# Seven block products in place of eight in the gate and up stages of a two-layer decoder trunk

## The chip, the cores and the metric

One core of one Trainium2 chip runs the whole program. The metric is device time in microseconds of one execution; three runs of the kernel before have a median of 978.27 us. All tensors are float32 in memory. The engines named below are TensorE (PE, matmuls, and PEld for its weight loads), VectorE (DVE), ScalarE (ACT), GpSimd (POOL) and SyncE (SP, which issues the weights' loads). Each engine works through its own instructions in the order in which the program emits them; semaphores hold an instruction until what it reads is there.

## What is computed

The reference is a trunk of two layers over 256 tokens of width 1024. Each layer is: half a gated feed-forward, a mixer (attention, short convolution and a recurrent branch), and half a second gated feed-forward, each behind an RMS norm. What matters here is the feed-forward:

```python
def swiglu(x, w_gate, w_up, w_down):        # w_gate, w_up: 1024 x 2816
    return (jax.nn.silu(x @ w_gate) * (x @ w_up)) @ w_down
...
h = x + 0.5 * swiglu(rms_norm(x, ffn1_norm[l]), ffn1_gate[l], ffn1_up[l], ffn1_down[l])
```

There are four of these (two in each layer), so four gate and up stages. The mixer's attention adds a relative bias whose table is spread over rows by a round trip through device memory.

## The kernel before

**Halves.** A float32 matmul is made of three fast ones: every operand is held as a high part, rounded to the matmul's format, and the remainder as a low part. `high` (L159) copies a weight piece to its high part on ACT, `low` (L164) subtracts on DVE. `mm3` (L203) issues the three matmuls. A piece is 512 KB, 128 x 1024 elements, loaded by SP into one of RAW = 6 buffers; PARTS = 7 pairs of high and low parts exist, so the splitting runs up to seven pieces ahead of TensorE.

**Order.** `pump` (L184) is called after each piece is used and calls `split` (L175): the high part of piece n, then the low part of piece n - 1. What is emitted for DVE after a `pump` thus stands behind the low parts of pieces that TensorE needs only six or seven pieces later.

**A gate and up stage** (`up_gate`, L300) has eleven units, each of 256 hidden columns: 256 gate columns and 256 up columns side by side, so 512 columns a matmul. A unit takes four pieces, each with 12 matmuls (two rows of 128 tokens, two blocks of 128 inputs, three products), 48 in all. After its last piece, `gate` (L313) forms silu(gate) on ACT and the product on DVE (L319), both scaled by the norm's factor of the token, since the matmuls take the input without that factor. `turn` (L324) transposes the result on TensorE (four transposes, L328) and splits it (ACT L330, DVE L331). It stands after the second piece of the next unit: TensorE comes to these transposes 24 matmuls after the unit's end.

**The norm's factor** is formed at the end of unit 0 (`ssq`, L243). In the first stage `ssq` stands in unit 2.

**Bias rows.** In the first stage `skew_out(i)` (L462, a copy of 384 KB from two partitions to device memory) and `skew_in(i)` (L470, back in another order) are issued on ACT's queue, after units 6 to 10: after unit 6 + i the copy out number i and the copy in number i - 1. A copy in waits for its copy out, and ACT's other work waits behind it.

Of the kernel before, what the change touches and what calls it, by code (L numbers as in the profile page):

```python
# [17 lines left out]
P = 128  # L18
DEPTH = 2
S = 256  # L20
# [10 lines left out]
RAW = 6  # L31
# [21 lines left out]
UNITS = KF // 2  # L53

# [16 lines left out]
def trunk(ctx: ExitStack, tc: tile.TileContext, t, out):  # L71
# [48 lines left out]
    pieces = []  # L120

    def four(w):

        pieces.extend((w[:, 0:4], w[:, 4:8]))

    for l in range(DEPTH):
        for f in ("ffn1", "ffn2"):
            pieces.extend(t[f"{f}_gu{l}"][i] for i in range(4 * UNITS))
            w = t[f"{f}_down{l}"]
            if l == DEPTH - 1 and f == "ffn2":  # L130
                pieces.extend(w[c, :, j:j + 1] for c in range(KF // 2) for j in range(2))
            else:
                pieces.extend(w[n, :, k0:k1] for n in range(4) for k0, k1 in DOWN_K)
# [6 lines left out]
    st = {"dma": 0, "split": 0, "low": 0, "use": 0, "done": 0}  # L140
    raws, parts = {}, {}

    def load(i, cut=1, before=None):
        src = pieces[i]
        r = raw_p.tile([P, src.shape[1], src.shape[2]], F32, tag="raw", name=f"raw{i}")
# [6 lines left out]
        raws[i] = r  # L152
        st["dma"] += 1

    def load_more():
        while st["dma"] < min(len(pieces), st["low"] + RAW):
            load(st["dma"])

    def high(i, s):  # L159
        if i not in parts:  # L160
            parts[i] = tuple(hl_p.tile(list(raws[i].shape), F32R, tag=g, name=f"{g}{i}") for g in ("wh", "wl"))
        nc.scalar.activation(out=parts[i][0][:, s], in_=raws[i][:, s], func=AF.Copy)  # L162

    def low(i, s):  # L164
        h, lo = parts[i]
        nc.vector.tensor_tensor(out=lo[:, s], in0=raws[i][:, s], in1=h[:, s].bitcast(F32), op=ALU.subtract)  # L166

    def low_to(n):
        while st["low"] < n:
            low(st["low"], slice(None))  # L170
            raws.pop(st["low"])
            st["low"] += 1
            load_more()

    def split():  # L175

        n = st["split"]
        if n >= len(pieces):
            return
        high(n, slice(None))  # L180
        st["split"] += 1
        low_to(n)

# [19 lines left out]
    def mm3(o, ah, al, bh, bl, first, last):  # L203
        nc.tensor.matmul(o, lhsT=ah, rhs=bh, start=first, stop=False)  # L204
        nc.tensor.matmul(o, lhsT=ah, rhs=bl, start=False, stop=False)  # L205
        nc.tensor.matmul(o, lhsT=al, rhs=bh, start=False, stop=last)  # L206
# [20 lines left out]
    def rows(o, w, k, ds):  # L227

        for d in ds:
            wh, wl = w[d // 2]  # L230
            mm3(o, xh[:, d, tok(k)], xl[:, d, tok(k)], wh[:, d % 2], wl[:, d % 2], d == 0, d == KD - 1)
# [68 lines left out]
    def up_gate(norm, first, hooks=()):  # L300

        hooks = dict(hooks)
        hid, tiles = [], []
        for j, n in enumerate((10, 8, 4)):
            tile_ = big.tile([P, n, 2, S], F32R, tag=f"A{j}", name=f"hid{j}")
            tiles.append((len(hid), tile_))
            hid += [tile_[:, k] for k in range(n)]

        def hidden(c):
            k0, tile_ = [x for x in tiles if x[0] <= 2 * c][-1]  # L310
            return tile_[:, 2 * c - k0:2 * c - k0 + 2]

        def gate(b):  # L313
            s = wk.tile([P, 2, 256], F32, tag="sg", name="sg")
            a = wk.tile([P, 2, 256], F32, tag="ga", name="ga")
            for k in range(2):
                nc.scalar.activation(out=s[:, k], in_=b[k][:, :256], func=AF.Silu, scale=norm.r[:, k:k + 1])  # L317
            for k in range(2):
                nc.vector.scalar_tensor_tensor(  # L319
                    out=a[:, k], in0=b[k][:, 256:], scalar=norm.r[:, k:k + 1], in1=s[:, k], op0=ALU.mult, op1=ALU.mult  # L320
                )
            return a

        def turn(c, a):  # L324
            b = bank("hT")
            for j in range(2):
                for k in range(2):
                    nc.tensor.transpose(b[:, (2 * j + k) * P:(2 * j + k + 1) * P], a[:, k, tok(j)], ident)  # L328
# [10 lines left out]
        for c in range(UNITS):  # L339
            b = pair("n")  # L340
            banks.append((c, b))
            if first and c == 0:
                start(b)
            else:
                for j in range(4):
                    w = [None] * j + take(1)
                    if j < 3 or c > 0:
                        for k in range(2):
                            rows(b[k], w, k, (2 * j, 2 * j + 1))
                    else:  # L350
                        for k in range(2):
                            rows(b[k], w, k, (KD - 2,))
                        rows(b[0], w, 0, (KD - 1,))
                        norm.ssq()
                        rows(b[1], w, 1, (KD - 1,))
# [5 lines left out]
                    if j > 0:  # L361
                        turn_next()
                    pump()
                    if first and c == 2 and j == 1:
                        gated += [(i, gate(o)) for i, o in banks[:2]]
                        banks = banks[2:]
            if not first or c > 1:
                gated += [(i, gate(o)) for i, o in banks]
                banks = []
            if c in hooks:  # L370
                hooks[c]()
        return hid, turn_next

    def ffn(norm, first, gain, hooks=()):
        hid, last = up_gate(norm, first, hooks)
        for n in range(4):
            acc = pair("d")
            for k0, k1 in DOWN_K:
                w = take(1)[0]
                for i in range(2):  # L380
                    c = slice(i * P, (i + 1) * P)
                    for k in range(k0, k1):
                        wide(acc[i], w[0][:, k - k0, c], w[1][:, k - k0, c], hid[k], k == 0, k == KF - 1)
# [3 lines left out]
                if n == 0 and k0 == 8:  # L387
                    last()
# [87 lines left out]

    def skew(i):
        def go():
            if i < 4:
                skew_out(i)  # L480
            if i > 0:
                skew_in(i - 1)
        return go
# [315 lines left out]
    for j in range(4):  # L799
        load(j, 2, lambda: load_x(j))  # L800
# [7 lines left out]
    def start(b):  # L808
# [3 lines left out]
        for j in range(4):  # L812
# [7 lines left out]
            raws.pop(j)  # L820
            parts.pop(j)
            st["use"] = st["split"] = st["low"] = st["done"] = j + 1
            load_more()
# [11 lines left out]
    ffn(norm, True, ("mix_norm", 0), once | {6 + i: skew(i) for i in range(5)})  # L835
    for l in range(DEPTH):
# [3 lines left out]
        if l < DEPTH - 1:  # L840
            ffn(norm, False, ("ffn1_norm", l + 1))
            norm = Norm()
            ffn(norm, False, ("mix_norm", l + 1))


    xn = big.tile([P, 2, D], F32, tag="A3", name="xn")

    def turn_back(k, n):
        def go():
            b = bank("xn")  # L850
            for i in range(4):
                nc.tensor.transpose(b[:, i * P:(i + 1) * P], xT[:, 4 * n + i, k * P:(k + 1) * P], ident)
            nc.scalar.activation(out=xn[:, k, n * 512:(n + 1) * 512], in_=b, func=AF.Copy)
        return go

    hid, turn_last = up_gate(norm, False, {2 + 2 * k + n: turn_back(k, n) for k in range(2) for n in range(2)})
# [7 lines left out]
    def row(k, n, w, d):  # L864
        c0, c1 = cuts[k][n]
        mm3(
            acc[k][n][:, :c1 - c0], hid[d][:, 0, tok(k)], hid[d][:, 1, tok(k)], w[0][:, 0, c0:c1], w[1][:, 0, c0:c1],
# [32 lines left out]
    for d in range(KF - 4):  # L900
# [5 lines left out]
        if d == 8:  # L906
            turn_last()
        pump()
# [17 lines left out]
def paired(g, u):  # L926

    both = np.concatenate([w.reshape(KD // 2, 2, P, UNITS, 256).transpose(3, 0, 2, 1, 4) for w in (g, u)], axis=-1)
    return np.ascontiguousarray(both.reshape(4 * UNITS, P, 2, 512))
# [34 lines left out]
```

## Time and profile before

| | |
|---|---|
| median of three runs | 978.27 us (977.99 to 981.36) |
| the profiled execution | 978.68 us, span 976.5 us |
| TensorE busy | 955.3 us, 98% of the span |
| VectorE busy | 581.4 us, 60% |
| ScalarE busy | 506.7 us, 52% |
| matmuls on TensorE | 5350 |

Busy shares are means over stages. Times below are microseconds from the start of the span; a matmul's shown duration is longer than the distance to the next one, because matmuls overlap.

### The profile page before, as it was taken

The page shows a single profiled execution, that of the slowest core. Times are in us where ns is not written, and L with a number is a line of the kernel's source. Part 1 is how long each engine was busy: PE and PEld are TensorE (multiplying, and loading weights), DVE is VectorE, ACT ScalarE, POOL GpSimd, SP SyncE. Part 2 cuts the span into 40 slices and gives each one's busy share as a digit, 9 for nine tenths or more (in the row PEclk, how much of TensorE's full clock was granted, in tenths as well). Part 3 has the DMA queues.
Part 4 walks back from the last instruction along what each step waited for, and adds up shares of the span by engine and source line. Part 5 has one row for each costly group of instructions (what it writes and reads, how often), then busy time and mean ns, then how long its engine had stood idle before and what let it go on. Part 6 is the DMA issues. An engine that isn't in the chain of part 4 may idle for free.

```text
span 976.5 us, 13921 instructions
## 1 busy us (share of the span) xinstructions
PE 955.3 (98%) x5350; PEld 830.9 (85%) x5350; DVE 581.4 (60%) x812; ACT 506.7 (52%) x775; POOL 24.1 (2%) x46
## 2 busy tenths in 40 slices
PE   8999969999999999999999999999999999999997
PEld 7788757899999888888888888888999988888886
DVE  6655425667788555555665555465778765555543
ACT  7555324556776544444544544444587655544441
POOL 0002000000000000000000000000001000000000
PEclk9999989999999999999999999999999999999999
DMA  8855447654445555646565555556444465555621
GB/s 308 271 179 197 145 146 215 222 170 171 138 143 200 198 188 187 205 152 195 169 220 181 185 173 183 162 187 221 159 143 157 160 210 192 183 182 182 221 93 44
DMA packets 53045, 176.64 MB, mean 181 GB/s; under 512 B 6867, under 2 KB 8948, under 8 KB 52980
## 3 DMA queue, kind: packets, MB, share of 16 engines
q1 hardware_dynamic: 48960, 171.46, 53.0%
q10 hardware_dynamic: 4020, 4.30, 1.5%
q8 instruction: 42, 0.69, 0.3%
q14 instruction: 23, 0.19, 0.1%
HBM read 173.11 MB, written 2.62 MB: 180 GB/s over the span
## 4 chain that ended last, share of the span: by engine, by line
PE 91%; DMA 6%; issue 1%; ACT 1%; ACTq 0%; DVE 0%; POOLq 0%; POOL 0%; SPq 0%
PE nb L204 8%; PE na L206 8%; PE na L204 8%; PE na L205 8%; PE nb L206 8%; PE nb L205 8%; PE da L221 6%; PE db L221 6%; DMA skew<-br 5%; PE da L222 3%; PE db L222 3%; PE hT L328 2%; PE v L204 1%; PE q L205 1%; PE wb L205 1%; PE wb L204 1%
## 5 line engine op out<-in xcount | busy, mean ns | idle before, releaser
L162 ACT ACTIVATE wh<-raw 128x1024 fp32r<-128x1024 f32 (+1 forms) x334 | 339.2, 1030 | 296.8 <-PE nb L206 106.9
L166 DVE TENSOR_TENSOR wl<-raw,wh 128x1024 fp32r<-128x1024 f32 (+1 forms) x334 | 387.9, 1187 | 66.7 <-ACT wh L162 66.7
L204 PE MATMUL na<-wh,xx 128*128 128x512 f32 x352 | 142.1, 404 | 1.4 <-ACT wh L162 1.4
L206 PE MATMUL na<-wh,xx 128*128 128x512 f32 x352 | 138.2, 393 | 0.0
L205 PE MATMUL na<-wl,xx 128*128 128x512 f32 x352 | 137.9, 392 | 0.2 <-DVE wl L166 0.2
L204 PE MATMUL nb<-wh,xx 128*128 128x512 f32 x352 | 137.9, 392 | 0.0
L206 PE MATMUL nb<-wh,xx 128*128 128x512 f32 x352 | 137.4, 390 | 0.0
L205 PE MATMUL nb<-wl,xx 128*128 128x512 f32 x352 | 137.4, 390 | 0.0
L331 DVE TENSOR_TENSOR hid<-hT,hid 128x512 fp32r<-128x512 f32 x44 | 30.4, 692 | 150.2 <-ACT hid L330 150.2
L221 PE MATMUL da<-hid,wh 128*128 128x512 f32 x252 | 92.4, 399 | 1.5 <-DVE hid L331 1.5
L221 PE MATMUL db<-hid,wh 128*128 128x512 f32 x252 | 92.1, 398 | 0.0
L204 PEld LDWEIGHTS na<-wh,xx 128*128 128x128 f32 x352 | 66.6, 189 | 14.3 <-ACT wh L162 1.6
L206 PEld LDWEIGHTS na<-wh,xx 128*128 128x128 f32 x352 | 66.5, 189 | 14.3
L205 PEld LDWEIGHTS nb<-wl,xx 128*128 128x128 f32 x352 | 66.4, 189 | 14.0
L206 PEld LDWEIGHTS nb<-wh,xx 128*128 128x128 f32 x352 | 66.4, 189 | 14.1
L204 PEld LDWEIGHTS nb<-wh,xx 128*128 128x128 f32 x352 | 66.4, 189 | 13.9
L205 PEld LDWEIGHTS na<-wl,xx 128*128 128x128 f32 x352 | 66.7, 190 | 12.8 <-DVE wl L166 0.5
L222 PE MATMUL da<-hid,wl 128*128 128x256 f32 x252 | 70.7, 280 | 0.0
L222 PE MATMUL db<-hid,wl 128*128 128x256 f32 x252 | 70.6, 280 | 0.0
L330 ACT ACTIVATE hid<-hT 128x512 fp32r<-128x512 f32 x44 | 26.2, 595 | 80.2 <-PE hT L328 80.2
L319 DVE SCALAR_TENSOR_TENSOR ga<-na,rr,sg 128x256 f32<-128x256 f32 x44 | 21.3, 483 | 75.3 <-ACT sg L317 75.3
L221 PEld LDWEIGHTS da<-hid,wh 128*128 128x128 f32 x252 | 47.4, 188 | 12.8 <-DVE hid L331 1.9
(282 smaller groups left out, 1519.7 us busy)
## 6 DMA issues: line engine op xcount, KB each, us to landing
raw<-in_ffn_gu SPq DMA_DIRECT2D x172, 512.0 KB, 4.3
raw<-in_ffn_down SPq DMA_DIRECT2D x82, 512.0 KB, 4.2
raw<-in_w_in SPq DMA_DIRECT2D x44, 512.0 KB, 4.3
raw<-in_w_out SPq DMA_DIRECT2D x16, 512.0 KB, 4.8
raw<-in_ffn_down SPq DMA_DIRECT2D x12, 256.0 KB, 2.7
raw<-in_ffn_gu SPq DMA_DIRECT2D x8, 256.0 KB, 5.0
skew<-br ACTq DMA_DIRECT2D x4, 384.0 KB
xT<-in_x SPq DMA_DIRECT2D x4, 256.0 KB, 4.9
```

Source lines behind the costliest of these rows:

```text
L162: nc.scalar.activation(out=parts[i][0][:, s], in_=raws[i][:, s], func=AF.Copy)
L166: nc.vector.tensor_tensor(out=lo[:, s], in0=raws[i][:, s], in1=h[:, s].bitcast(F32), op=ALU.subtract)
L204: nc.tensor.matmul(o, lhsT=ah, rhs=bh, start=first, stop=False)
L205: nc.tensor.matmul(o, lhsT=ah, rhs=bl, start=False, stop=False)
L206: nc.tensor.matmul(o, lhsT=al, rhs=bh, start=False, stop=last)
L221: nc.tensor.matmul(o, lhsT=wh, rhs=flat(v), start=first, stop=False)
L222: nc.tensor.matmul(o[:, :S], lhsT=wl, rhs=v[:, 0], start=False, stop=False)
L319: nc.vector.scalar_tensor_tensor(out=a[:, k], in0=b[k][:, 256:], scalar=norm.r[:, k:k + 1], in1=s[:, k], op0=ALU.mult, op1=ALU.mult)
L328: nc.tensor.transpose(b[:, (2 * j + k) * P:(2 * j + k + 1) * P], a[:, k, tok(j)], ident)
L330: nc.scalar.activation(out=h[:, :, 0], in_=two(b), func=AF.Copy)
L331: nc.vector.tensor_tensor(out=h[:, :, 1], in0=two(b), in1=h[:, :, 0].bitcast(F32), op=ALU.subtract)
```

## The change

In each stage two pairs of units (units 5 and 6 and units 9 and 10 in the first stage, 3 and 4 and 7 and 8 in the others) are formed by `seven`: the 256 x 1024 input and the pair's 1024 x 1024 weights (512 gate columns, 512 up columns) are cut into 2 x 2 blocks, and seven block products stand in place of eight. Of each product's weights there are two pieces, with six matmuls each. Four of the seven weight blocks are sums, made on DVE in place (`add`); the others are plain. The sums of the products are formed on DVE and ACT while the pair runs. `norm_all` makes a normed input with its halves, `blocks` the input's sums with theirs; units from number `normed` on read the normed input. The other seven units of a stage are as before. `spread` is now called in every gate and up stage, as it was in the mixers. The copies of the bias rows are issued after units 3 to 6 (out) and 7 to 10 (in); where a pair covers two units, the copies of both are issued at its end. RAW is 7, and sums have two buffers of their own.

```diff
+PLANS = {True: ("11111" "2" "11" "2", 4), False: ("111" "2" "11" "2" "11", 2)}
...
+    def group(w):
+        b11 = [source(w[i], "sum") for i in range(2)]
+        b12, b22, b21 = ([source(w[2 * j + i]) for i in range(2)] for j in (1, 2, 3))
+        for key, other in (
+            (b11, None), (b11, b12), (b12, b22), (b11, b22), (b22, None), (b21, None), (b11, b21),
+        ):
+            forms.extend((key[i], other and other[i]) for i in range(2))
...
+    def add(i):
+        if st["sum"] > i or i >= len(forms):
+            return
+        key, other = forms[i]
+        if other is not None:
+            nc.vector.tensor_tensor(out=raws[key], in0=raws[key], in1=raws[other], op=ALU.add)
+            used(other)
+        st["sum"] += 1
...
     def split():
...
+        add(n)
         high(n, slice(None))
         st["split"] += 1
         low_to(n)
+        add(n + 1)
...
+        def halves_of(o, v):
+            for j in range(2):
+                d = slice(4 * j, 4 * j + 4)
+                nc.scalar.activation(out=o[:, d, 0], in_=v[:, d], func=AF.Copy)
+            for j in range(2):
+                d = slice(4 * j, 4 * j + 4)
+                nc.vector.tensor_tensor(out=o[:, d, 1], in0=v[:, d], in1=o[:, d, 0].bitcast(F32), op=ALU.subtract)
+
+        def norm_all():
...
+            for d in range(KD):
+                nc.vector.scalar_tensor_tensor(
+                    out=xn[:, d], in0=xT[:, d], scalar=par(gain[0], gain[1] * KD + d), in1=norm.R,
+                    op0=ALU.mult, op1=ALU.mult,
+                )
+            halves_of(xx2, xn)
...
+        def blocks():
...
+            nc.vector.tensor_tensor(out=a22, in0=a21, in1=a22, op=ALU.subtract)
+            nc.vector.tensor_tensor(out=a21, in0=a11, in1=a21, op=ALU.subtract)
+            nc.vector.tensor_tensor(out=a11, in0=a22, in1=a11, op=ALU.subtract)
+            nc.vector.tensor_tensor(out=a12, in0=a12, in1=a11, op=ALU.add)
+            halves_of(xx, xn)
...
+            def product(o, v, first, after=()):
+                more = {} if first else {"skip_group_check": True}
+                for j in range(2):
+                    wh, wl = take(1)[0]
+                    for i in range(2):
+                        k = 2 * j + i
+                        mm3(o, v[:, k, 0], v[:, k, 1], wh[:, i], wl[:, i], first and k == 0, k == 3, **more)
+                    done(1)
+                    if j < len(after):
+                        after[j]()
+                    pump()
...
+            product(p, a11, True, (turn_next,))
+            nc.scalar.activation(out=x[0], in_=p, func=AF.Copy)
+            product(q, s1, True)
+            nc.scalar.activation(out=x[1], in_=q, func=AF.Copy)
+            product(r, s3, True)
+            product(u, s2, True)
...
+            nc.vector.tensor_tensor(out=x[0], in0=x[0], in1=u, **add_)
+            nc.vector.tensor_tensor(out=x[2], in0=x[0], in1=r, **add_)
+            nc.vector.tensor_tensor(out=x[1], in0=x[1], in1=x[2], **sub)
+            product(q, s4, False)
+            nc.vector.tensor_tensor(out=x[2], in0=q, in1=x[0], **sub)
+            product(p, a12, False)
...
+            nc.scalar.activation(out=x[3], in_=p, func=AF.Silu)
+            nc.vector.tensor_tensor(out=x[2], in0=x[2], in1=x[3], op=ALU.mult)
+            product(r, a22, False)
+            nc.vector.tensor_tensor(out=x[0], in0=x[0], in1=r, **add_)
+            nc.scalar.activation(out=x[0], in_=x[0], func=AF.Silu)
+            nc.vector.tensor_tensor(out=x[1], in0=x[1], in1=x[0], op=ALU.mult)
...
+        for kind in plan:
+            if kind == "2":
+                seven(c)
+                for i in (c, c + 1):
+                    if i in hooks:
+                        hooks[i]()
+                c += 2
+                continue
...
+                    if c == normed - 1 and j == 0:
+                        norm.spread()
+                        norm_all()
+                    if c == normed and j == 1:
+                        blocks()
...
-    ffn(norm, True, ("mix_norm", 0), once | {6 + i: skew(i) for i in range(5)})
+    for i in range(4):
+        once[3 + i] = (lambda i, old: lambda: (old and old(), skew_out(i)))(i, once.get(3 + i))
+        once[7 + i] = lambda i=i: skew_in(i)
```

The transposes of the trunk's input that stood inside the last stage (`turn_back`) move behind it, unchanged in number.

## Rows read from the trace of the kernel before

**Rows 1.** The page's first part: busy time, share, instructions of each engine.

```profile
PE 955.3 (98%) x5350; PEld 830.9 (85%) x5350; DVE 581.4 (60%) x812; ACT 506.7 (52%) x775; POOL 24.1 (2%) x46
```

**Rows 2.** Waits, 95 to 170 us: total us, times, longest us.

```profile
PE hT L328 <- DVE ga L319: 10.1, 2, 7.9
PE da L221 <- DVE hid L331: 1.5, 1, 1.5
```

**Rows 3.** The chain that ended last, whole span: start us, us, what.

```profile
50.27 0.44 PE hT L328 x4
...
72.97 0.44 PE hT L328 x4
...
221.73 0.45 PE rb L259 x4
...
326.92 0.44 PE hT L328 x4
338.27 0.44 PE hT L328 x4
349.62 0.44 PE hT L328 x4
```

**Rows 4.** DVE in order of time, second stage: start us, us, instructions.

```profile
324.41 0.48 DVE L319 SCALAR_TENSOR_TENSOR ga<-na,rr,sg 128x256 f32<-128x256 f32 x1 [2.44 <-ACT sg L317]
324.81 0.48 DVE L319 SCALAR_TENSOR_TENSOR ga<-nb,rr,sg 128x256 f32<-128x256 f32 x1
325.20 1.22 DVE L166 TENSOR_TENSOR wl<-raw,wh 128x1024 fp32r<-128x1024 f32 x1
328.02 0.69 DVE L331 TENSOR_TENSOR hid<-hT,hid 128x512 fp32r<-128x512 f32 x1 [1.60 <-ACT hid L330]
328.63 2.35 DVE L166 TENSOR_TENSOR wl<-raw,wh 128x1024 fp32r<-128x1024 f32 x2
...
335.10 1.22 DVE L166 TENSOR_TENSOR wl<-raw,wh 128x1024 fp32r<-128x1024 f32 x1
```

**Rows 5.** Groups by line, shapes kept apart: busy us, mean ns, idle before.

```profile
L166 DVE TENSOR_TENSOR wl<-raw,wh 128x1024 fp32r<-128x1024 f32 x314 | 374.4, 1219 | 66.2 <-ACT wh L162 66.2
...
L281 DVE SCALAR_TENSOR_TENSOR xx<-xT,pc,xx 128x256 fp32r<-128x256 f32 x40 | 19.4, 484 | 13.2 <-ACT xx L278 13.2
...
L523 DVE TENSOR_TENSOR yt<-mxt,yt 128x512 fp32r<-128x512 f32 x4 | 2.8, 688 | 1.4 <-ACT yt L522 1.4
```

**Rows 6.** Stretches of 3 us: PE, PEld, DVE, ACT, POOL, PEclk, DMA, GB/s.

```profile
108.00:111.00 3.00, 3.00 (x15) 2.47 (x14) 0.00 (x0) 0.00 (x0) 0.00 (x0) 1.00 0.19 75
...
135.00:138.00 3.00, 0.00 (x0) 0.00 (x0) 2.17 (x3) 3.00 (x5) 0.00 (x0) 0.84 0.37 116
138.00:141.00 3.00, 0.63 (x2) 0.42 (x3) 3.00 (x5) 1.36 (x3) 0.00 (x0) 0.50 0.57 131
141.00:144.00 3.00, 3.00 (x10) 2.49 (x10) 0.84 (x1) 0.00 (x0) 0.00 (x0) 0.52 0.43 158
```

**Rows 7.** DVE in order of time, first stage, after unit 3.

```profile
58.46 0.16 DVE L419 TENSOR_SCALAR ab<-pc 128x4 f32<-128x4 f32 x1
...
59.59 1.22 DVE L166 TENSOR_TENSOR wl<-raw,wh 128x1024 fp32r<-128x1024 f32 x1
```

**Rows 8.** ACT's queue in order of time: the bias rows' copies, duration of issue.

```profile
90.38 0.75 ACTq L468 DMA_DIRECT2D skew<-br  x1
...
112.31 2.10 ACTq L472 DMA_DIRECT2D bias<-skew  x1
...
127.35 6.80 ACTq L472 DMA_DIRECT2D bias<-skew  x1
...
143.68 7.00 ACTq L472 DMA_DIRECT2D bias<-skew  x1
...
160.62 0.39 ACTq L472 DMA_DIRECT2D bias<-skew  x1
```

More of the change, by code (lines that the diff above doesn't have):

```diff
@@ L138, in trunk, with load @@
                     four(t[f"w_out{l}"][c])
-    st = {"dma": 0, "split": 0, "low": 0, "use": 0, "done": 0}
+    st = {"dma": 0, "sum": 0, "split": 0, "low": 0, "use": 0, "done": 0}
     raws, parts = {}, {}
-    def load(i, cut=1, before=None):
-        src = pieces[i]
-        r = raw_p.tile([P, src.shape[1], src.shape[2]], F32, tag="raw", name=f"raw{i}")
+    room = {"raw": RAW, "sum": 2}
+    left = [0] * len(sources)
+    for key, other in forms:
+        left[key] += 1
+        if other is not None:
+            left[other] += 1
+    def load(cut=1, before=None):
+        i = st["dma"]
+        src, tag = sources[i]
+        r = raw_p.tile([P, src.shape[1], src.shape[2]], F32, tag=tag, name=f"{tag}{i}", bufs=2 if tag == "sum" else RAW)
         step = src.shape[1] // cut
@@ L298, in part, with up_gate, gate @@
         )
-    def up_gate(norm, first, hooks=()):
+    def up_gate(norm, first, gain, hooks=()):
         hooks = dict(hooks)
[L303 to L307, printed above, removed]
-        def hidden(c):
-            k0, tile_ = [x for x in tiles if x[0] <= 2 * c][-1]
+        plan, normed = PLANS[first]
+        tiles = []
+        def hidden(c):
+            while 2 * c >= sum(n for _, n, _ in tiles):
+                j = len(tiles)
+                k0, n = ((0, 10), (10, 8), (18, 4))[j]
+                tiles.append((k0, n, big.tile([P, n, 2, S], F32R, tag=f"A{j}", name=f"hid{j}")))
+            k0, _, tile_ = [x for x in tiles if x[0] <= 2 * c][-1]
             return tile_[:, 2 * c - k0:2 * c - k0 + 2]
-        def gate(b):
+        def gate(b, scaled):
             s = wk.tile([P, 2, 256], F32, tag="sg", name="sg")
@@ L354, in up_gate @@
                         norm.ssq()
+                        norm.diagonal()
                         rows(b[1], w, 1, (KD - 1,))
@@ L360, in up_gate @@
                         norm.ssq()
-                    if j > 0:
+                        norm.diagonal()
+                    if c == normed - 1 and j == 0:
[3 more added lines that the diff above has]
+                        blocks()
+                    if j > 0 and not (first and c == 2 and j == 2):
                         turn_next()
@@ L371, in up_gate, with place, ffn @@
                 hooks[c]()
-        return hid, turn_next
-    def ffn(norm, first, gain, hooks=()):
-        hid, last = up_gate(norm, first, hooks)
+            c += 1
+        def place(k):
+            return hidden(k // 2)[:, k % 2]
+        return place, turn_next
+    def ffn(norm, first, own_gain, gain, hooks=()):
+        hid, last = up_gate(norm, first, own_gain, hooks)
         for n in range(4):
@@ L819, in start @@
                     rows(b[k], [parts[j]] * 4, k, (d,))
-            raws.pop(j)
             parts.pop(j)
-            st["use"] = st["split"] = st["low"] = st["done"] = j + 1
-            load_more()
+            st["use"] = st["split"] = st["low"] = st["done"] = st["sum"] = j + 1
+            used(j)
     def first_squares():
```

170 lines of the change are left out of this document (112 added, 58 removed).

## The prediction

> **What bounds the kernel now.** The page's first part was read first: TensorE is busy for 955.3 of 976.5 us [rows 1], so only fewer matmuls, or TensorE's few waits, can make this kernel faster. Next the chain that ended last, for the pitch of the stage that is changed. In the second stage the transposes of consecutive units begin at 326.92, 338.27 and 349.62 [rows 3]: 11.35 us a unit. Less 0.44 for the four transposes [rows 3], 48 matmuls take 10.91 us, or 0.2273 us each. Then DVE in order of time, since the change gives it the new work. A low part recurs every 1.17 us (2.35 for two), the second part of `turn` fills 0.61 (328.02 to 328.63), each half of `gate` 0.40 (324.41, 324.81, 325.20) [rows 4]. In a unit that is 4 x 1.17 + 0.61 + 2 x 0.40 = 6.1 of 11.35 us: DVE has 5.2 us to spare in a unit, and no more. Last the waits of TensorE between 95 and 170 us, where the bias rows are copied: 10.1 + 1.5 = 11.6 us [rows 2]. After the longest one the granted clock falls to 0.50 (1.2 of 2.4 GHz), and 10 matmuls start in 3 us where 15 did [rows 6], so that 5 x 0.2273 = 1.1 us more are lost. I count 12.7 us for this place.
>
> **What the change takes off TensorE.** A pair has 84 matmuls in place of 96: 12 x 0.2273 = 2.73 us, 5.46 in a stage, 21.8 in all. `spread` adds 0.45 us [rows 3] to each stage. The copies of the bias rows get four units between out and in, so the old wait for a copy out goes: -12.7.
>
> **What it puts on DVE.** No row shows a sum of weights. It has the elements and operands of a low part (two inputs of 128 x 1024 in SBUF, mean 1219 ns [rows 5]), so I take 1.17 us; its bounds are 0.61 (the group of half the size, 688 ns, less the overlap) and 1.22. A normed input block costs like the scaled halves of 128 x 256 (484 ns [rows 5]), 0.40 in sequence; a 512-element sum 0.61 to 0.69 [rows 5].
>
> What decides is not the sum over a stage but one place: the transposes of the unit ahead of a pair. They stood 24 matmuls behind that unit's end; in `seven` they stand behind the pair's first piece, 6 matmuls or 1.36 us. They need `gate` of that unit, and in DVE's order `gate` stands behind everything that `pump` emitted, which now reaches seven pieces into the pair, sums too. TensorE's matmuls behind the transposes wait with them, although their pieces are ready; the old wait of TensorE on L319 is of this kind [rows 2].
>
> The ledger for the second stage, from 325.20, where DVE has finished `gate` of unit 0 [rows 4], to the end of `gate` of unit 2:
>
> - eight low parts (pieces 10 to 17): 9.4
> - six sums, of the pair's third to eighth pieces, emitted one piece ahead of their high parts: 7.0
> - `norm_all`: 8 x 0.40 + 2 x 1.17 = 5.5
> - `blocks`: 4 x 0.61 + 2 x 1.17 = 4.8
> - `turn` twice, `gate` twice: 1.2 + 1.6
> - DVE idle until ACT has the high part of `blocks`: between 0 and 1.0, I take 0.5.
>
> That is 30.0 us, so `gate` of unit 2 ends at 355.2. TensorE comes to the transposes at 349.62 - 24 x 0.2273 = 344.16 (start of unit 3 before), plus 0.45, plus 1.36 = 346.0. It waits 9.2 us. Behind a wait of this length the clock fell [rows 6]: 1.1 more.
>
> At the second pair of a stage DVE has caught up: from the end of that wait it has 22 low parts, 8 sums, 7 sums of products, 4 `turn` and 2 `gate`, 43.5 us, and TensorE 42.7 (0.44 + 13 x 1.364 + 2 x 10.91 + 3 x 0.44 + 1.36) until the next such transposes. A floor remains without any lateness: `gate` of unit 1 ended at 335.10 [rows 4], 2.3 us after the unit's end (338.27 - 5.46 = 332.81), 1.0 more than the 1.36 us that the pair gives. With DVE's 0.8 and its waits for ACT inside the pair, I take 1.5, between 1.0 and 2.4.
>
> A stage of the second kind: -5.46 + 0.45 + 9.2 + 1.1 + 1.5 = +6.8. Three: +20.4.
>
> The first stage has the same ledger later. The norm is spread after the first piece of unit 3, whose start is 50.27 - 5.46 = 44.81 [rows 3]; with that piece (2.73), `spread` and about 0.4 for ACT's copy DVE begins `norm_all` at 48.4. The ledger of 30.0 and `exponents` (58.46 to 59.59, 1.1 [rows 7]) end at 79.5. TensorE is there at 72.97 - 5.46 + 0.45 + 1.36 = 69.3: a wait of 10.2. The stage: -5.46 + 0.45 + 10.2 + 1.1 + 1.5 - 12.7 = -4.9.
>
> **The copies that move.** The four copies out and in occupy 90.38 to about 160.6 [rows 8], 17.6 us for each copy out, beside loads. What held ACT was not only the wait: the copy in issued at 127.35 took 6.80 us to issue and the one at 143.68 took 7.00, each with a younger copy out ahead of it on the queue, and the last, with none, 0.39 [rows 8]. I read this as: ACT can hand over no further copy until the one ahead has run for some 7 us. Two copies out now stand back to back at the first pair's end, and copies in behind them. The pair: 79.5 + 0.44 + 13 x 1.364 = 97.7 on TensorE; ACT gets there when DVE has done 14 low parts, 2 sums, 6 sums of products and a `turn` from 79.5 on (23.1 us), and a silu of 0.5 behind them, at 103.1. Copy out 2 is handed over at once (0 and 1, issued at 56.6 and 68, are through by 92). Copy out 3 is held to 103.1 + 7 = 110.1. ACT then has four high parts, two copies of `turn` and a `gate` in front of unit 7's result, which DVE ends near 118; TensorE's transposes were due at 97.7 + 10.9 + 0.9 + 5.5 = 115.0: a wait of 3. Copy in 0, behind `gate` of unit 7, is held until copy out 3 has run 7 us: 103.1 + 17.6 + 7 = 127.7. Behind it on ACT are four high parts of the second pair, each with a sum and a low part on DVE, and `gate` of unit 8: 127.7 + 9.4 + 0.6 + 0.8 = 138.5, and some 0.4 of hand-overs. TensorE wants that `gate` at 118 + 0.44 + 5.46 + 1.36 = 125.3. It waits 13.6 in place of 1.5. Sum: +15.1, and 1.1 for the clock: +16.2. The bounds are 0 (ACT hands on at once, as at 160.62) and 20 (each hold 2 us longer).
>
> A rule speaks to this price. The row shows 0.19 of the DMA engines busy and 75 GB/s while almost nothing but a copy out ran [rows 6]: few of sixteen engines carry it. The Trainium skill, page DMA: Bandwidth & Descriptors, section Why a DMA increments its semaphore by 16 and not by 1, says that a transfer is split over the largest count up to 16 that divides the outermost dimension of both sides; that dimension is 2 here, so two engines, with which the row agrees. With the some 27 GiB/s for an engine of its Specifications, 384 KB would take an estimated 6.8 us, by which the copies would be through before ACT comes to the next one, and the sum would be the one without +16.2. I keep 17.6 us, which holds beside loads.
>
> **Sum.** The profiled execution took 978.7 us, 0.4 above the median, which is nothing here. 978.7 + 20.4 - 4.9 + 16.2 = 1010.4. I predict 1010 us.
>
> **The rivals.**
>
> *The copies don't hold ACT.* All else as above: 994 us. For it: copy out issues themselves took 0.75 us [rows 8], and none was seen behind one just begun. Against it: the 6.80 and 7.00. The figure of the Trainium skill's DMA page, above, would lead here.
>
> *Faster: DVE isn't late at the first pair.* Then its wait is like the second's 1.5: a stage gains 5.46 - 0.45 - 3.0 = 2.0, four of them 8.0, and with the old wait gone the time is 978.7 - 8.0 - 12.7 = 958 us. It turns at this wait: without clock loss and with copies that cost nothing, four stages of (s - 3.5) against 12.7 come out even at s = 6.7 us. The ledger would have to be 2.5 us shorter, each of six sums 0.75 us rather than 1.17. For it: DVE is busy for 60% of the span only, and 5.2 us a unit are free. Against it: what is free in two units, 10.4, is less than the 17.3 of sums, `norm_all` and `blocks`. With no wait at the pairs at all: 978.7 - 21.8 + 1.8 - 12.7 = 946.
>
> *Even.* A first wait near 6.7, or a cheaper ledger with copies that hold ACT for a few microseconds: 974 to 983.
>
> **How the numbers follow.** The forecast 0.42 (its own range 1000 to 1025), the copies free 0.34, even 0.06, faster 0.18 (some of it at 946). The range 970 to 1025 leaves out most of the faster case (0.15) and 0.04 above. A measurement of this kernel tells 0.5% (4.9 us) from no change: faster 0.18, same 0.06, slower 0.76.
>
> **What would show it.** Matmuls fall from 5350 by 96, plus those of four `spread`. TensorE's waits on `gate` (L319 before) should be the longest of the page: four of 8 to 11 us at the first pairs, smaller ones at the second. In the second stage DVE should have no gap between units 1 and 2. On ACT's queue the second copy out at the first pair's end should take about 7 us to issue, and the first copy in more than 8. The prediction is wrong if the sums take clearly under 1 us each, if the transposes' wait at the first pairs stays under 6 us, or if pieces and not `gate` are what the pairs wait for.

## The result, and the profile after

The changed kernel takes 1023.93 us (median of four runs, 1018.24 to 1024.73) against 979.19 us for the kernel before (median of four): a ratio of 1.0437, 95% interval 1.0399 to 1.0476. It is slower by 44.7 us; the time lies 13.9 us above the forecast of 1010 and inside the range that was given (970 to 1025). The profiled execution is the shortest of the four, 1018.24 us: its span is 39.8 us longer than before, a little less than what the median lost.

The page's first part (busy time, share, instructions) and the shares of the chain that ended last, to be read against [rows 1]:

```profile
PE 947.6 (93%) x5270; PEld 819.6 (81%) x5270; DVE 771.4 (76%) x1020; ACT 569.6 (56%) x843; POOL 25.6 (3%) x46
...
PE 68%; DVE 20%; issue 6%; ACT 4%; ACTq 1%; DMA 0%; DVEq 0%; POOLq 0%; POOL 0%
```

The matmuls fell from 5350 to 5270: 96 went, and four calls of `spread` with four each came. TensorE's busy time fell only by 7.7 us where these matmuls are worth 20.0 (96 x 0.2273 less 4 x 0.45); the other 12.3 us are matmuls that took longer. Most of this is the clock: busy time times what the granted clock lacks of 1.00, summed over windows of 3 us, is 10.5 us here and 3.4 before, 7.1 more. The remaining 5 are not accounted for. DVE's busy time rose by 190 us, and DVE now holds a fifth of the chain (0% before). What it holds up is in the view of TensorE's waits over the whole span (total us, times, longest us), for which [rows 2] has the stretch from 95 to 170 us before:

```profile
PE hT L396 <- DVE ga L389: 50.7, 9, 10.0
PE hT L396 <- DVE x L482: 9.4, 7, 1.7
...
PE hT L396 <- DVE ga L384: 0.5, 3, 0.2
```

The same view of the kernel before has more than the stretch of [rows 2]:

```profile
PE hT L328 <- DVE ga L319: 11.0, 3, 7.9
...
PE na L204 <- ACT wh L162: 1.4, 1, 1.4
```

L396 is `turn`, L389 the product of `gate` for units that read the normed input, L482 the last product of a pair's results. The wait on L389 is the forecast one. By place it is 10.0 us at the first stage's first pair, 8.2 at each of the three others, 9.5 at the first stage's second pair, 1.7 at the others' second pairs and 1.5 in unit 8. The wait on L482 was not forecast: it falls in the unit behind a pair, where the transposes of the pair's own results come after the second and third piece (385.02 us is 24 matmuls behind the pair's end in the second stage). The bill of the profiled execution, over the whole span: the waits shown and 0.7 in smaller rows are 61.3, less 14.1 before (these two rows, the 1.5 of [rows 2] and 0.2), +47.2 (the same 1.0 us at the very start is left out of both); matmuls and `spread` -20.0; together +27.2 of 39.8. The remaining 12.6 agree with the 12.3 of the longer matmuls.

The place of the ledger, DVE in order of time in the second stage (start us, us, instructions; the bracket is idle time ahead and its releaser), against [rows 4]:

```profile
329.52 0.47 DVE L384 SCALAR_TENSOR_TENSOR ga<-nb,rr,sg 128x256 f32<-128x256 f32 x1
...
345.00 1.22 DVE L211 TENSOR_TENSOR raw<-raw,raw 128x1024 f32<-128x1024 f32 x1
346.14 0.68 DVE L435 TENSOR_TENSOR xnorm<-xnorm 128x512 f32<-128x512 f32 x1
...
349.40 2.36 DVE L416 TENSOR_TENSOR xx<-xnorm,xx 128x1024 fp32r<-128x1024 f32 x2 [0.40 <-ACT xx L413]
...
355.69 1.22 DVE L211 TENSOR_TENSOR sum<-sum,raw 128x1024 f32<-128x1024 f32 x1
356.82 1.22 DVE L223 TENSOR_TENSOR wl<-raw,wh 128x1024 fp32r<-128x1024 f32 x1
357.96 1.22 DVE L211 TENSOR_TENSOR sum<-sum,raw 128x1024 f32<-128x1024 f32 x1
359.09 0.41 DVE L389 TENSOR_TENSOR ga<-na,sg 128x256 f32<-128x256 f32 x1
359.43 0.41 DVE L389 TENSOR_TENSOR ga<-nb,sg 128x256 f32<-128x256 f32 x1
```

A sum of weights (L211) takes 1.22 us and is followed by the next instruction after 1.13 to 1.14: a low part's time, as taken. From 352.28 low parts and sums alternate up to `gate` (L389); from 345.00 on there is one gap, of 0.40. TensorE in the same place, in order of time:

```profile
359.56 1.24 PE L396 MATMUL hT<-ident,ga 128*128 128x128 f32 x4 [8.15 <-DVE ga L389]
360.45 0.78 PE L264 MATMUL s<-wh,xx 128*128 128x512 f32 x1
...
363.15 0.45 PE L264 MATMUL s<-wh,xx 128*128 128x512 f32 x1
```

The transposes wait 8.15 us for `gate` and then take 0.89 (359.56 to 360.45) where 0.44 is usual; six matmuls take 2.70 us (to 363.15) where six take 1.36. The windows of 3 us (columns as in [rows 6]) show why:

```profile
351.00:354.00 3.00, 0.41 (x2) 0.00 (x0) 3.00 (x4) 0.75 (x1) 0.00 (x0) 1.00 0.00 0
354.00:357.00 3.00, 0.00 (x0) 0.00 (x0) 3.00 (x4) 1.06 (x1) 0.00 (x0) 0.91 0.04 11
357.00:360.00 3.00, 0.44 (x2) 0.29 (x3) 2.84 (x4) 1.60 (x3) 0.00 (x0) 0.50 0.73 253
360.00:363.00 3.00, 3.00 (x10) 2.52 (x10) 1.54 (x2) 1.55 (x2) 0.00 (x0) 0.50 0.21 86
363.00:366.00 3.00, 3.00 (x14) 2.39 (x14) 2.67 (x4) 2.50 (x3) 0.00 (x0) 0.95 0.00 0
```

The clock falls to 0.50 (1.2 of 2.4 GHz) during the wait, with TensorE idle, and is back around 363. From these rows the loss is 0.45 + 1.34 = 1.8 us, not the 1.1 of the sum.

Last the copies, ACT and its queue in order of time, against [rows 8]:

```profile
102.03 5.55 ACTq L636 DMA_DIRECT2D skew<-br  x2
107.70 1.06 ACT L219 ACTIVATE wh<-raw 128x1024 fp32r<-128x1024 f32 x1 [5.05 <-DMA raw<-in_ffn_gu]
...
114.30 10.21 ACTq L640 DMA_DIRECT2D bias<-skew  x1
...
124.61 1.06 ACT L219 ACTIVATE wh<-sum 128x1024 fp32r<-128x1024 f32 x1 [8.79 <-issue]
```

The two copies out that stand together take 5.55 us to issue, and the first copy in 10.21. Apart from what it had begun and two short instructions, over at 115.82, ACT does nothing else in that time; the next high part begins only at 124.61. Seven and "more than 8" were forecast. Where the idle time ahead of 107.70 is put down to a load, ACT's queue itself was held until 107.58.

### The profile page after: what moved, and what is told of

It reads as the page before. It is cut to its first block, busy times and chain, and to the rows that moved or that the text cites. A ratio compares the mean times of both kernels' runs of the same rounds, so it can differ in the third digit from the quotient of the medians.

```text
span 1016.3 us, 13936 instructions
## 1 busy us (share of the span) xinstructions
PE 947.6 (93%) x5270; PEld 819.6 (81%) x5270; DVE 771.4 (76%) x1020; ACT 569.6 (56%) x843; POOL 25.6 (3%) x46
## 4 chain that ended last, share of the span: by engine, by line
PE 68%; DVE 20%; issue 6%; ACT 4%; ACTq 1%; DMA 0%; DVEq 0%; POOLq 0%; POOL 0%
DVE wl L223 9%; PE db L281 6%; PE da L281 6%; PE da L282 3%; PE db L282 3%; PE nb L264 3%; PE na L265 3%; PE na L264 3%; PE na L266 3%; PE nb L266 3%; PE s L264 3%; PE nb L265 2%; PE s L265 2%; PE s L266 2%; ACT wh L219 2%
## 5 line engine op out<-in xcount | busy, mean ns | idle before, releaser
L219 ACT ACTIVATE wh<-raw 128x1024 fp32r<-128x1024 f32 (+1 forms) x318 | 319.9, 1027 | 173.4 <-PE db L281 54.9
L223 DVE TENSOR_TENSOR wl<-raw,wh 128x1024 fp32r<-128x1024 f32 (+1 forms) x318 | 369.2, 1185 | 59.9 <-ACT wh L219 59.0
L219 ACT ACTIVATE wh<-sum 128x1024 fp32r<-128x1024 f32 x64 | 67.4, 1058 | 65.1 <-DVE sum L211 49.2
L264 PE MATMUL s<-wh,xx 128*128 128x512 f32 x224 | 91.6, 409 | 0.0
L264 PE MATMUL na<-wh,xx 128*128 128x512 f32 x224 | 90.7, 405 | 0.5 <-ACT wh L219 0.5
L265 PE MATMUL s<-wl,xx 128*128 128x512 f32 x224 | 89.9, 401 | 0.0
L266 PE MATMUL s<-wh,xx 128*128 128x512 f32 x224 | 89.7, 400 | 0.0
L264 PE MATMUL nb<-wh,xx 128*128 128x512 f32 x224 | 87.7, 391 | 0.0
L265 PE MATMUL na<-wl,xx 128*128 128x512 f32 x224 | 87.4, 390 | 0.2 <-DVE wl L223 0.2
L266 PE MATMUL na<-wh,xx 128*128 128x512 f32 x224 | 87.5, 391 | 0.0
L266 PE MATMUL nb<-wh,xx 128*128 128x512 f32 x224 | 87.4, 390 | 0.0
L265 PE MATMUL nb<-wl,xx 128*128 128x512 f32 x224 | 87.2, 389 | 0.0
L223 DVE TENSOR_TENSOR wl<-sum,wh 128x1024 fp32r<-128x1024 f32 x64 | 77.2, 1217 | 0.6
L396 PE MATMUL hT<-ident,ga 128*128 128x128 f32 x112 | 22.5, 315 | 51.5 <-DVE ga L389 50.7
L396 PEld LDWEIGHTS hT<-ident,ga 128*128 128x128 f32 x112 | 14.6, 154 | 60.9 <-DVE ga L389 55.4
L211 DVE TENSOR_TENSOR sum<-sum,raw 128x1024 f32<-128x1024 f32 x48 | 58.5, 1219 | 0.5
L281 PEld LDWEIGHTS db<-hid,wh 128*128 128x128 f32 x252 | 47.4, 188 | 11.3
```

The lines of the kernel that those rows point to most:

```text
L211: nc.vector.tensor_tensor(out=raws[key], in0=raws[key], in1=raws[other], op=ALU.add)
L219: nc.scalar.activation(out=parts[i][0][:, s], in_=r[:, s], func=AF.Copy)
L223: nc.vector.tensor_tensor(out=lo[:, s], in0=raws[forms[i][0]][:, s], in1=h[:, s].bitcast(F32), op=ALU.subtract)
L266: nc.tensor.matmul(o, lhsT=al, rhs=bh, start=False, stop=last, **more)
L281: nc.tensor.matmul(o, lhsT=wh, rhs=flat(v), start=first, stop=False)
```

## The experiments

Two theories stood against each other after the result. *DVE is late*: at each first pair everything that DVE makes is late, whatever TensorE asks for, because of the sums of weights. *The place*: only the transposes are late, since they stand behind `gate` and too early in the pair; the pieces are ready. Beside both, the copies hold ACT and cost some 11 to 16 us. The first four kernels were timed beside a median of 979.71 us of the kernel before, the next four beside 980.61, the last two beside 980.87.

**The sums of weights left out** (the products then use plain blocks in place of sums, so part of the computation is missing).

```diff
         if other is not None:
-            nc.vector.tensor_tensor(out=raws[key], in0=raws[key], in1=raws[other], op=ALU.add)
             used(other)
```

> The changed kernel without the in-place sums of weights on VectorE: four of the seven weight blocks are left as loaded, so their products are of other blocks; every other instruction stays. Theory (VectorE's ledger ahead of the gate): the ledger ahead of the first pair is 7.0 us shorter, so the four longest waits of TensorE (10.0, 8.2, 8.2, 8.2 us) fall to between 1.2 (all of it) and 4.5 us (if VectorE instead waits for ScalarE's high parts), the clock holds there, and the waits on the result of a pair (9.4 us in all) shrink to under 3; 985 to 1000 us. Rival 1 (the pairs wait for loads or for TensorE's own order): the waits stay above 7 us and the time above 1015. Rival 2 (the copies' holds on ScalarE are the main part): only the first stage changes, above 1010.

970.91 us, ratio 0.9906 (0.9888 to 0.9925), below what was expected. TensorE's waits of this kernel (L388 is the unscaled `gate`):

```profile
PE hT L395 <- DVE ga L388: 18.4, 9, 8.0
```

The first pairs' waits are 1.7 to 2.9 us in place of 8.2 to 10.0, those on the pair's results are gone, and the 8.0 is the one behind the copies. So 64 sums, 73 us of DVE's time, cost 53.0 us of the kernel's 1023.9. It is shown that without them DVE is hardly late: most of the waits at first pairs go, all waits on results, and part of the longer matmuls (TensorE is busy for 942.5 us in place of 947.6). `norm_all` and `blocks`, 10.3 us of the same ledger, were not taken out by themselves.

**The transposes ahead of a pair put behind its seventh piece** instead of its first.

```diff
-            product(p, a11, True, (turn_next,))
+            product(p, a11, True)
...
-            product(u, s2, True)
+            product(u, s2, True, (turn_next,))
```

> The changed kernel with the transposes of the unit ahead of a pair moved from behind the pair's first piece to behind its seventh (36 more matmuls in between). Theory that only the place of the transposes is at fault (the pieces behind them are ready, as the prediction said): all waits on gate and their clock losses go, some 49 us less waits of 50.7 and 9 of clock, time 965 to 975. Theory that VectorE is late with everything, gate first: the wait on gate goes, but the same lateness comes back as waits on low parts (wl) and on sums of products inside the first pair, some 6 to 9 us a stage in several small waits, so that about 3 us a stage and the clock's 2 are gained: 1000 to 1010.

1006.05 us, ratio 1.0266 (1.0249 to 1.0283): 17.9 us less than the changed kernel, not the 50 that the place alone would give. TensorE's waits:

```profile
PE s L265 <- DVE wl L223: 13.0, 12, 2.7
PE s L264 <- DVE x L471: 11.8, 4, 3.3
PE hT L396 <- DVE x L482: 11.0, 6, 2.1
PE s L264 <- ACT wh L219: 3.3, 1, 3.3
```

The wait on `gate` is gone but for 0.5 us. In its place TensorE waits for low parts (L223) and for sums of results (L471), which stood behind `gate` before and are late too, and once, by this view, for a high part (L219). With the early place TensorE waits once, for long; with the late place often, and less in all. The waits of the whole span are 41.1 us in place of 61.3. "DVE is late" holds, with the time in its range of 1000 to 1010, and the place is the smaller part as long as DVE is late.

**The copies apart**: the last copy out after unit 7, all four copies in after the last unit.

```diff
-        once[7 + i] = lambda i=i: skew_in(i)
+    once[6] = None
+    once[7] = lambda: skew_out(3)
+    once[10] = lambda: [skew_in(i) for i in range(4)]
...
```

> The changed kernel with the bias rows' copies moved once more: copy out 3 after unit 7 in place of right behind copy out 2, and all four copies in behind the second pair. Theory (a copy that stands behind one just begun holds ScalarE): the issues of 4.90 and 10.21 us on ScalarE's queue go to under 2 us ahead of the second pair; the first stage's wait of 9.5 us ahead of its second pair falls to the 1.7 of the other stages and the 1.5 in unit 8 goes, 9.3 us, and some 2 of clock: 11 us less than the changed kernel on this chip. Rival (VectorE alone makes that wait): the time stays within 3 us of the changed kernel's.

1013.72 us, ratio 1.0345 (1.0325 to 1.0365): 10.2 us less than the changed kernel. ACT's queue in order of time, and TensorE's wait on `gate` from 112 to 150 us:

```profile
75.54 0.67 ACTq L636 DMA_DIRECT2D skew<-br  x1
...
104.15 0.61 ACTq L636 DMA_DIRECT2D skew<-br  x1
...
113.27 0.61 ACTq L636 DMA_DIRECT2D skew<-br  x1
...
150.44 2.05 ACTq L640 DMA_DIRECT2D bias<-skew  x4
```
```profile
PE hT L396 <- DVE ga L389: 1.7, 1, 1.7
```

No issue is held now: 0.61 to 0.67 for a copy out, 2.05 for four copies in. The first stage's second pair waits 1.7 us in place of 9.5, like the others, and the wait in unit 8 has gone.

**The change of the copies alone, in the kernel before**: the same four units between out and in, or the places of the experiment just told.

```diff
-    ffn(norm, True, ("mix_norm", 0), once | {6 + i: skew(i) for i in range(5)})
+    for i in range(4):
+        once[3 + i] = (lambda i, old: lambda: (old and old(), skew_out(i)))(i, once.get(3 + i))
+        once[7 + i] = lambda i=i: skew_in(i)
+    ffn(norm, True, ("mix_norm", 0), once)
```

> The kernel before with nothing but the change's places for the bias rows' copies (out after units 3 to 6, in after units 7 to 10). Theory of the wait alone: the waits of 11.6 us and 1.9 of clock go, 965 us. Theory of the hold: a copy out fills the queue for 17.6 us but one is issued every 11.35, so copy out 3 is held some 7 us and copy in 0 some 10 or more, TensorE still waits 2 to 8 us around units 8 and 9, 968 to 974 us.

978.11 us, ratio 0.9978 (0.9962 to 0.9993): 1.6 us gained of the 12.7 that the prediction took off for the old wait, and slower than both theories expected.

> The kernel before with nothing but the copies apart: copies out after units 3, 4, 5 and 7, all copies in after unit 10. Theory of the hold: no copy stands behind one just begun but copy out 2 (some 6 us, covered by the seven pieces ahead), so the waits of 7.7 us that e4_copies_alone still has around units 8 and 9 go too: 964 to 970. Rival (the copies cost TensorE its time by sharing the loads' way): no faster than e4_copies_alone, 975 to 980.

With the places apart 974.99 us, ratio 0.9931 (0.9914 to 0.9949): 5.6 us, not the 964 to 970 of the hold alone and at the edge of the rival's 975 to 980. ACT and its queue in this second kernel, the waits of the loads' queue (SP) from 20 to 170 us, and a window (columns as in [rows 6]):

```profile
78.86 6.14 ACTq L468 DMA_DIRECT2D skew<-br  x1
105.28 1.06 ACT L162 ACTIVATE wh<-raw 128x1024 fp32r<-128x1024 f32 x1 [7.78 <-DMA raw<-in_ffn_gu]
...
122.15 1.06 ACT L162 ACTIVATE wh<-raw 128x1024 fp32r<-128x1024 f32 x1 [10.22 <-DMA raw<-in_ffn_gu]
```
```profile
SPq L151 <- DMA skew<-br: 24.9, 3, 11.7
```
```profile
93.00:96.00 3.00, 3.00 (x17) 2.48 (x17) 0.58 (x1) 0.90 (x2) 0.00 (x0) 1.00 0.11 28
```

One copy out is still held (6.14 us, the third, 11.3 us behind the second), and beside the copies out ACT waits 7.78 and 10.22 us for pieces of weights. These loads come late because they are issued late: SP stands still for up to 11.7 us until a copy out has ended, by its view, and from 87 to 96 us the DMA engines are busy for 0.11 to 0.13 only, so that no lack of engines holds the loads up. In the first of these kernels SP waits 35.3 us for copies out, in the kernel before 20.3. Why an issue of SP waits for a copy out stays open. TensorE's waits of before are thus not removed by distance alone: of the 11.6 us between 95 and 170 us [rows 2], 7.7 are left in the first of these kernels and 5.7 in the second. (The first has a wait of 4.2 us at 36 to 48 us too, ahead of all copies, where the kernel before has 0.8.)

**Another plan, which gives DVE time before the pair, with the copies apart.** In the three later stages the pairs move from units 3 and 4 and 7 and 8 to units 5 and 6 and 9 and 10, so that three units lie between `norm_all` and the first pair; in the first stage the norm is spread a unit earlier. Once with the transposes behind the first piece as in the change, once behind the seventh.

```diff
-PLANS = {True: ("11111" "2" "11" "2", 4), False: ("111" "2" "11" "2" "11", 2)}
+PLANS = {True: ("11111" "2" "11" "2", 3), False: ("11111" "2" "11" "2", 2)}
```

> As e5_plan_late_apart, but with the transposes behind the pair's first piece as in the change. Theory: the floor of the wait on gate (1.0 to 2.4 us a pair, eight pairs) stays, 12 to 18 us more than e5_plan_late_apart with little clock lost: 962 to 970. If the place of the transposes costs nothing once VectorE is on time: within 3 us of e5_plan_late_apart.

985.24 us, ratio 1.0045 (1.0031 to 1.0059): more than expected. Its waits:

```profile
PE hT L396 <- DVE ga L389: 18.5, 9, 3.8
PE hT L396 <- DVE x L482: 5.8, 4, 1.7
PE hT L396 <- DVE ga L384: 3.0, 1, 3.0
```

> The changed kernel with three edits: all four stages in the order of the first one (five units, a pair, two units, a pair), so that two more units stand between the normed input and the first pair, and the normed input one unit earlier in the first stage; the transposes ahead of a pair behind the pair's seventh piece; the copies as in e3_copies_apart. Theory (VectorE is late only where norm_all, blocks and six sums meet in two units): two more units give it 10.4 us, the 9 us of lateness are gone by the first pair, a stage takes about 121 us where the kernel before took 124.8, and the copies cost nothing: 978 - 4 x 3.5 - 13 = 950, within 945 to 958, faster than the kernel before. Rival (a pair by itself is bound by VectorE, wherever it stands): waits on low parts and on sums of products inside the pairs as in e2_late_turn, above 970.

965.5 us, ratio 0.9832 (0.9811 to 0.9854): faster than the kernel before by 1.7%, which is less than expected.

```profile
PE hT L396 <- DVE x L482: 6.8, 4, 2.1
PE s L264 <- DVE x L471: 3.5, 1, 3.5
```

The plan took 28.5 us off the version with only the copies apart (1013.72). The place of the transposes, worth 17.9 us while DVE was late everywhere, is worth 19.7 now that DVE keeps up. The profiled executions are 17.9 us apart; 15.3 of these are waits (29.2 to 13.9 over all rows), and 2.7 are TensorE's busy time, for which no cause is shown, since the mean granted clock is 0.990 in both. The clock answers to short waits too; windows of the second kernel behind a wait of 2.1 us:

```profile
381.00:384.00 3.00, 1.52 (x8) 0.97 (x6) 2.30 (x4) 0.82 (x2) 0.00 (x0) 1.00 1.02 410
384.00:387.00 3.00, 2.41 (x8) 1.96 (x9) 2.87 (x4) 2.30 (x3) 0.00 (x0) 0.68 1.02 415
387.00:390.00 3.00, 3.00 (x14) 2.41 (x13) 0.63 (x1) 0.05 (x1) 0.00 (x0) 0.75 0.95 321
```

**The sums on GpSimd**, which is idle for 97% of the span. The edit moves all 64 sums: the 48 of the expectation are one of two groups, and 16 more are formed in the load buffers.

```diff
-            nc.vector.tensor_tensor(out=raws[key], in0=raws[key], in1=raws[other], op=ALU.add)
+            nc.gpsimd.tensor_tensor(out=raws[key], in0=raws[key], in1=raws[other], op=ALU.add)
```

> The changed kernel with the 48 sums of weights on GpSimd in place of VectorE. Theory: VectorE's ledger is 7.0 us shorter ahead of the first pair, as in e1_no_sums (971), provided that GpSimd makes a sum of 128 x 1024 in under some 2.7 us (one piece of a plain unit) and does not slow VectorE: 970 to 985. If GpSimd takes longer, or VectorE's two-input instructions slow beside it, the pairs wait for the sums instead: above 1010. No trace here has a GpSimd instruction of that size.

1064.51 us, ratio 1.0841 (1.0822 to 1.0859). A group of POOL (busy us, mean ns), and POOL and DVE in order of time in the second stage:

```profile
L211 POOL TENSOR_TENSOR sum<-sum,raw 128x1024 f32<-128x1024 f32 x48 | 144.4, 3025 | 219.6 <-DVE wl L223 141.4 <-issue 28.9 <-ACT wh L219 25.1
```
```profile
352.98 5.73 POOL L211 TENSOR_TENSOR raw<-raw,raw 128x1024 f32<-128x1024 f32 x2
...
352.98 3.47 DVE L223 TENSOR_TENSOR wl<-sum,wh 128x1024 fp32r<-128x1024 f32 x1
356.38 2.88 DVE L435 TENSOR_TENSOR xnorm<-xnorm 128x512 f32<-128x512 f32 x1
```

A sum takes 3.03 us on GpSimd, and a low part that runs beside one takes 3.47 us in place of 1.22, a sum of half that size (`blocks`) 2.88 in place of 0.69. DVE's busy time did not fall (781.1 us against 771.4), and TensorE's waits on `gate` grew to 71.4 us.

**The turns behind a pair one piece later**, on the version with the other plan, the late turn ahead of a pair and the copies apart: after the third and fourth piece of the unit behind a pair. The expectation counts them one too low: in the trace the transposes move from 24 and 36 matmuls behind the pair's end to 36 and 48.

```diff
-        c = 0
+        c, behind = 0, None
...
+                behind = c + 2
                 seven(c)
...
-                    if j > 0 and not (first and c == 2 and j == 2):
+                    if j > (c == behind) and not (first and c == 2 and j == 2):
```

> The version with the other plan, the late turn ahead of a pair and the copies apart (965.5 us), with one thing more: the unit right behind a pair turns the pair's results after its second and third pieces, not after its first and second. If the remaining waits of TensorE on the pair's results (6.8 us in four places, longest 2.1) are a matter of place, they go, and with them some of the clock lost behind them (about 1 to 2 us each in the places where it fell): 955 to 961 us, and no wait of TensorE on the pair's results over 1 us. If DVE is late with the pieces behind these results as well, the waits come back at pieces or at gates, and the time stays within 3 us of 965.5.

956.18 us (955.22 to 956.75), ratio 0.9744 (0.9724 to 0.9764), the fastest of all. The page's first part and TensorE's waits:

```profile
PE 938.7 (98%) x5270; PEld 815.9 (86%) x5270; DVE 766.0 (80%) x1020; ACT 566.7 (59%) x843; POOL 25.6 (3%) x46
```
```profile
PE s L264 <- DVE x L471: 3.5, 4, 2.7
PE hT L396 <- DVE ga L384: 3.0, 1, 3.0
PE rb L320 <- DVE dg L315: 1.5, 1, 1.5
```

The waits on the pair's results have gone, and with them 9.3 us. The profiled executions are 10.4 us apart: 5.4 are waits (the 6.8 are gone, but the wait on L384 grew by 1.7; the rest is small), and 4.9 are TensorE's busy time, which agrees with the mean granted clock (0.995 for 0.990). The matmuls are those of the changed kernel, in 938.7 us in place of 947.6. DVE is busy for 80% of the span, and TensorE waits only 8.0 us for it.

**One pair in a stage** on the same version (plan "11111" "2" "1111" in all stages).

> As the run beside it, with one pair in a stage, not two: four pairs in all, at 2.73 less 0.45 us of matmuls each, 9.1 us. If each pair costs DVE's lateness about as much as it takes off TensorE, this version comes within 3 us of the one with two pairs, between 958 and 966 us. If the second pair is free of waits, as its place in a unit's worth of slack says, this version is slower by the second pair's 10.9 us less at most 2: 966 to 972 us.

965.65 us, ratio 0.9843 (0.9819 to 0.9866): 9.5 us more than with two pairs, so not the theory in which a pair costs what it saves (within 3 us). Four further pairs save 48 matmuls, worth 10.9 us: nearly all of that is kept once their place is right.

The steps from the change to the best version, in medians: 1023.93, copies apart 1013.72, plan 985.24, transposes ahead 965.50, turns behind 956.18. Not all that this gains on the kernel before is due to the seven products: that kernel with the copies apart takes 974.99, so the rest of the change (the pairs, their normed input, `spread`, the buffers) is worth 18.8 us, 1.9%, where matmuls less `spread` are worth 20.0.

## Why the prediction came out as it did

**Right: the sign, the cause and the place.** The ledger of 30.0 us began at 325.20 and ended at 355.2, with TensorE there at 346.0. In the trace `gate` of unit 0 is done at 329.91, and the ledger's low parts, sums and the rest fill DVE up to 359.84: 29.9 us. TensorE came at 351.41 (359.56 - 8.15). Both are some 5 us later than forecast, since the stage begins later, and the distance is 8.4 where 9.2 was worked out. The first stage's wait is 10.0 (10.2), the second pairs' 1.7 (1.5). The price of a sum, 1.17 by the low part, was 1.13 to 1.14. The rival in which DVE isn't late was given a small chance for the right reason (a pair's work does not fit into what is free in two units), and the run without the sums shows that they make DVE late.

**Right in kind, mis-sized: the copies.** Both copies out that stand together and the first copy in hold ACT, 4.9 (5.55 less the 0.61 to 0.67 of an undisturbed one) and 10.21 us, where 7 and about 10 were taken; the wait at the second pair is 9.5, not 13.6, in unit 8 1.5, not 3. The separated copies gave back 10.2 us against +16.2 in the sum. The estimate from the Trainium skill's figure (page DMA: Bandwidth & Descriptors, section Specifications), by which copies would be through in 6.8 us and hold nothing, is not borne out: a copy out whose issue began 11.8 us behind the one ahead was held for 5.70 us in the kernel before with the copies moved, and with the copies apart 28 to 43 GB/s moved from 87 to 96 us, on 0.11 to 0.13 of sixteen engines (about the two that the prediction took), by which 384 KB take an estimated 9 to 14 us. The measured times decide.

**Wrong: the -12.7 for the old wait.** The step "the old wait for a copy out goes" took the whole wait and its clock as won by distance. In the kernel before, with only the copies moved, 1.6 us came back, and 5.6 with the issues apart as well. The copies still hold ACT, and SP issues the next pieces late, since its issues wait for copies out too. The sum had no line for the second.

**Mis-sized: the clock.** The sum has 1.1 us behind each long wait, read from one window [rows 6]. The transposes and matmuls of the trace make it 1.8; for five such waits that is an estimated 9 us in place of 5.5. Behind a wait of 1.7 us, in the fourth stage, the clock was 0.50 as well (903 to 906 us), for which the sum had nothing. All in all the matmuls took 12.3 us longer than their number says, 7.1 of them by the granted clock of the windows. The granted clock of the other three runs is lower still (0.966 to 0.971 against 0.978), which goes with their 5.6 to 6.5 us more.

**Missed: the results of a pair.** The unit behind a pair transposes them after its second and third pieces, and the part-by-part account had no line for this: 9.4 us of waits. In the second stage the pair's matmuls end at 379.58 and the transposes begin 5.4 us later, but the last product of the results (L482) is done only at 386.4: its sums stand behind low parts in DVE's order (L480 starts at 384.37), and ACT's step between them takes another 0.7. The floor used for the second pair, `gate` 2.3 us behind a unit's end, holds for one step behind a unit and would not have shown this.

**Half right: "although their pieces are ready".** With the transposes put later, TensorE got 17.9 us back and then waited for low parts and sums of results. Some of the wait was the place; more was DVE's lateness, which no place hides.

The parts can be set against the profiled execution, 39.8 us of span where the sum has 31.7 (forecast, then measured): first pairs' waits 37.8, 34.6; the other second pairs 4.5, 5.1; the first stage's second pair and unit 8 16.6, 11.0; waits on results 0, 9.4; clock and longer matmuls 4.4, 12.6. The matmuls with `spread` (-20.0) came as forecast. The old waits (-11.6) are gone too, but only because what the copies cost now stands in the first stage's second pair and unit 8; small waits differ by -1.2. So the total came near with errors of both signs: waits at pairs and behind copies too dear by 8.2 together, results and clock too cheap by 17.6. That they partly cancel is luck. The other 5.7 us of the median are the profiled execution's lead over it.

## What to carry to other kernels

A product saved on the bound engine is paid for by the engine that forms its operands: count that engine's work between the first of it and the wait that ends last, not over a stage, and if it is late there, first give it units in between. Then look at each place where the bound engine turns to results just made: a change that is 4% slower became 2.6% faster by moving four things, with no operation taken out (0.7% of it the copies alone give the kernel before). A wait costs more than its length where the clock falls behind it, so several waits of 2 us are worth removing one by one.

## What the runs showed of the hardware

A sum of 128 x 1024 floats takes 3.03 us on GpSimd in the mean of 48, against 1.22 on VectorE. A low part of that size on VectorE took 3.47 us beside one, in place of 1.22; whether VectorE slows GpSimd was not measured. The granted clock showed 0.68 and 0.75 in windows behind a wait of 2.1 us, and 0.50 from 903 to 906 us of the changed kernel behind one of 1.7; behind other waits of 1.7 us there it stayed at 1.00, and what tells these apart stays open. A copy out of 384 KB on ACT's queue took 0.61 to 0.75 us to issue where it wasn't held, in the kernels with the copies moved, and where it was, 4.9 to 6.7 (a copy in of 256 KB up to 10.2); in that time ACT runs nothing of what stands behind the copy. The distance to the copy ahead alone doesn't settle it: the second of a row was not held 8.0 or 9.1 us behind the first, the third was 11.3 and 11.8 us behind the second.
